# Small operations of an attention from VectorE to ScalarE and GpSimd

## The chip, the cores and the metric

One core of a Trainium2 chip runs the whole kernel. Its engines are TensorE (PE in the profile; PEld is its weight load), VectorE (DVE), ScalarE (ACT), GpSimd (POOL) and SyncE (SP, which only starts transfers here). Each engine works through its own queue in order; the engines wait for each other through semaphores. The metric is the device time of one execution in microseconds, and lower is better.

## The reference

The kernel computes one decoder block for 512 positions of width 1024 in float32:

```python
h  = rmsnorm(x);  P = h @ W_in        # A: [B, C, x_in]; B: [q, k/v per branch, branch gates]; merge gates gA, gB
yA = B * causal_dwconv3(C * x_in)
yB = NSA(q, compressed / selected / window keys)
x  = x + W_o( sigmoid(gA) * (yA @ W_A) + sigmoid(gB) * (yB @ W_B) )
x  = x + W_down( silu(causal_dwconv3(W_g rmsnorm(x)) + b) * (W_u rmsnorm(x)) )
```

The attention (NSA) has 8 heads in 2 groups of 4. For each head three softmaxes are taken over the same query and added, each times a gate of its own (a sigmoid for each position, head and branch): one over compressed keys, one over selected blocks, one over a window. With 512 positions all blocks are selected and the window covers everything, so the last two are plain causal attentions. The compressed keys are blocks of 32 positions taken every 16 positions. A position sees a block that has ended at or before it:

```python
def masked_softmax(s, mask):
    p = jax.nn.softmax(jnp.where(mask, s, NEG), axis=-1)
    return jnp.where(mask, p, 0.0)
```

The first 31 positions see no block at all: all their scores are `NEG`, the softmax is even, and the second `where` makes it zero.

## The kernel before

**Products.** Every float32 operand of a large product is cut into a high part (a rounded copy, made by ScalarE) and a low part (what the rounding left). TensorE then adds three products: high by high, high by low, low by high. In the profile these are lines L420, L421 and L423 of the helper `dense`. The low part of a weight comes in one of three ways, chosen by `by` in `load_w` (L130 to L146): VectorE subtracts (`"vector"`), GpSimd subtracts (`"pool"`), or, with `"dma"`, ScalarE writes a negated copy of the high part and an accumulating transfer on GpSimd's queue adds the weight to it (`dma_split`, L165 to L170).

**Stages.** The token projections, the compressed keys and the preparation of queries and keys come first, then the attention with the short convolution and the merge gates between, then the output product, then the feed-forward part, which takes from about 370 us to the end.

**The attention.** `attend` runs for each pair of a query tile of 128 positions (tiles 3, 2, 1, 0) and a group of four heads: eight times. In each, TensorE makes the scores of each head (L639/L640; L665 for tile 0), VectorE adds the causal mask and takes the maximum (L691, L692), ScalarE takes exponentials with a running sum (L693), VectorE inverts the sums and multiplies them by the gates (`scale_of`, L642 to L644), ScalarE scales the exponentials (L699), VectorE transposes 32x32 blocks (L626), and two transfers on SyncE's queue carry them out to DRAM (`td_e`, L632) and back in transposed order (`tn_e`, L634). Then ScalarE and GpSimd split them into high (`ph`, L725) and low parts (L726), and TensorE multiplies them with the values (`po`, L728, L733). The tile for the exponentials (`e`) has two buffers, so a third use waits until the first has been read out.

**The compressed branch** sits between. Its scores for four heads and 32 blocks are gathered in `xc`, 128 positions x 128. VectorE takes the maximum (L704), subtracts it (L705), ScalarE takes the exponential (L706), VectorE sums (L707), inverts and multiplies by the gate (`scale_of`), GpSimd multiplies by a table of visible blocks `cm_one` (L709) and by the scale (L710), ScalarE makes the high part (L712), VectorE the low part (`xs`, L713), and TensorE transposes both (`ptc`, L716).

**Work between.** `conv_tile` (four times, three weights each: `wr_a`, `wh_a`, `wl_a`) and `mix_a_pair` and `gate_tile` (weights `wr_g` and `wr_ao`, low parts by GpSimd, L145) stand behind the attention in the text. They depend on little, and TensorE gets them as filling.

**Order.** The text gives only dependencies and priorities. A planner simulates the engines with its own costs when the kernel is built, and writes one fixed order for each queue, the queues of transfers among them. On the chip nothing is reordered: where a planned duration is not met, what stands behind waits. An edit can therefore move instructions of other parts, too.

Of the kernel before, what the change touches and what calls it, by code (L numbers as in the profile page):

```python
# [11 lines left out]
F32 = mybir.dt.float32  # L12
F32R = mybir.dt.float32r
I32 = mybir.dt.int32
AF = mybir.ActivationFunctionType
ALU = mybir.AluOpType
AX = mybir.AxisListType

P = 128
# [4 lines left out]
H = 8  # L24
# [61 lines left out]
def tile_block(ctx: ExitStack, tc: tile.TileContext, xT, pos, par, par2, w_tok, w_a3, w_gate, w_ao, w_bo, w_o,  # L86
# [13 lines left out]
    def const(shape, name, dt=F32, pool=sb):  # L100
        return pool.tile(shape, dt, name=name, tag=name)
# [262 lines left out]
                            pattern=[[-1, P]], channel_multiplier=1)  # L364
    cm_add = const([P, NT, NC], "cm_add", F32, pb)
    nc.gpsimd.memset(cm_add, 0.0)
    cm_one = const([P, NT, NC], "cm_one", F32, pb)
    nc.gpsimd.memset(cm_one, 1.0)
    for m, f in ((cm_add, NEG), (cm_one, 0.0)):
        nc.gpsimd.affine_select(out=m, in_=m, compare_op=ALU.is_ge, fill=f, base=-(CMPB - 1),  # L370
                                pattern=[[P, NT], [-STRIDE, NC]], channel_multiplier=1)
    mhalf = const([P, 12], "mhalf")
    nc.gpsimd.memset(mhalf, -0.5)

# [163 lines left out]
    def values(tt, acc):  # L538
        r = r1[:, tt:tt + 1]
        vv = acc[:, 0:256].rearrange("p (h d) -> p h d", d=HD)  # L540
        nc.scalar.activation(v_t[:, tt, :, 0:HD], vv, AF.Copy, scale=r)
        nc.vector.scalar_tensor_tensor(v_t[:, tt, :, HD:], vv, r, v_t[:, tt, :, 0:HD].bitcast(F32),
                                       op0=ALU.mult, op1=ALU.subtract)
        gt = gate_n[:, tt, :]
        nc.scalar.activation(gt, acc[:, 256:280], AF.Tanh, scale=r1h[:, tt:tt + 1])
        nc.vector.tensor_scalar(gt, gt, 0.5, 0.5, op0=ALU.mult, op1=ALU.add)

    kh = kHH.rearrange("p (b g) s -> p b g s", g=G)
    nc.gpsimd.tensor_copy(kh[:, 1, :, 0:NC], warm[:, 1:2, None].to_broadcast([P, G, NC]))
# [58 lines left out]
    def attend(pt_, g, qt):  # L608
# [32 lines left out]

        def scale_of(sums, br):  # L642
            nc.vector.reciprocal(sums, sums)
            nc.vector.tensor_mul(sums, sums, gates[:, :, br:br + 1])  # L644

        xc = small("xc", NC)
        if off == 0:
# [8 lines left out]
        if qt == 0:  # L656

            e = e_tile("", 2)
            mx = pt_.tile([P, HG, 2], F32, name=f"mx{tag}", tag="mx", bufs=1)
            sums = small("sums", 2)  # L660
            for i in range(HG):
                sc = s_bank(f"sc{tag}{i}")
                w = sc[:, 0:2 * (NC + P)].rearrange("p (b k) -> p b k", b=2)
                for j in range(2):
                    nc.tensor.matmul(w, q[:, g * HG + i, :], kk5[:, j, :, g, 0:NC + P], start=j == 0, stop=j == 1)  # L665
                nc.vector.tensor_add(xc[:, i, :], w[:, 0, 0:NC], cm_add[:, qt, :])
                dg = w[:, :, NC:]
                nc.vector.tensor_tensor(dg, dg, causal[:, None, :].to_broadcast([P, 2, P]), op=ALU.add)
                nc.vector.tensor_reduce(mx[:, i], dg, axis=AX.X, op=ALU.max, negate=True)
                for br in (1, 0):  # L670
                    nc.scalar.activation(e[:, :, br, i], dg[:, br].rearrange("p (b i) -> p b i", i=SQ), AF.Exp,
                                         bias=mx[:, i, br:br + 1], accum_out=sums[:, i, br:br + 1])
            nc.vector.reciprocal(sums, sums)
            nc.vector.tensor_mul(sums, sums, gates[:, :, 1:3])
            for br in (1, 0):
                nc.vector.tensor_tensor(e[:, :, br], e[:, :, br],
                                        sums[:, None, :, br:br + 1].to_broadcast([P, QB, HG, SQ]), op=ALU.mult)
            turned = turn(e, 2)
        for br in (1, 0):
            if qt > 0:  # L680
                o = off if br == 0 else 0
                e = e_tile(br, qt + 1)
                mx = small(f"mx{br}", 1)
                sums = small(f"sums{br}", 1)
                for i in range(HG):
                    sc = s_bank(f"sc{tag}{i}{br}")
                    scores(sc[:, 0:o + nk], i, br, NC - o, NC + nk)
                    if o:
                        nc.vector.tensor_add(xc[:, i, :], sc[:, 0:NC], cm_add[:, qt, :])
                    dg = sc[:, o + nk - P:o + nk]  # L690
                    nc.vector.tensor_add(dg, dg, causal)  # L691
                    nc.vector.tensor_reduce(mx[:, i], sc[:, o:o + nk], axis=AX.X, op=ALU.max, negate=True)  # L692
                    nc.scalar.activation(e[:, :, :, i].rearrange("p b k i -> p k b i"),  # L693
                                         sc[:, o:o + nk].rearrange("p (k b i) -> p k b i", b=QB, i=SQ), AF.Exp,
                                         bias=mx[:, i], accum_out=sums[:, i])
                scale_of(sums, 1 + br)
                for i in range(HG):
                    v = e[:, :, :, i]
                    nc.scalar.activation(v, v, AF.Copy, scale=sums[:, i])  # L699
                turned = turn(e, qt + 1)  # L700
            if br == 0:
                mcs = small("mcs", 2)
                mc, sc_ = mcs[:, :, 0:1], mcs[:, :, 1:2]
                nc.vector.tensor_reduce(mc[:, :, 0], xc, axis=AX.X, op=ALU.max)  # L704
                nc.vector.tensor_tensor(xc, xc, mc.to_broadcast([P, HG, NC]), op=ALU.subtract)  # L705
                nc.scalar.activation(xc, xc, AF.Exp)  # L706
                nc.vector.reduce_sum(sc_[:, :, 0], xc, axis=AX.X)  # L707
                scale_of(sc_, 0)
                nc.gpsimd.tensor_tensor(xc, xc, cm_one[:, qt, None, :].to_broadcast([P, HG, NC]), op=ALU.mult)  # L709
                nc.gpsimd.tensor_tensor(xc, xc, sc_.to_broadcast([P, HG, NC]), op=ALU.mult)  # L710
                xs = small("xs", 2 * NC, F32R)
                nc.scalar.activation(xs[:, :, 0:NC], xc, AF.Copy)  # L712
                nc.vector.tensor_sub(xs[:, :, NC:], xc, xs[:, :, 0:NC].bitcast(F32))  # L713
                pt = t_bank(f"ptc{tag}", 0)
                for a in range(2):
                    nc.tensor.transpose(pt[:, a * P:(a + 1) * P],  # L716
                                        xs[:, 2 * a:2 * a + 2, :].rearrange("p h c -> p (h c)").bitcast(F32), ident)
                pc = pt_.tile([P, 2, P], F32R, name=f"pc{tag}", tag="pc", bufs=1)
                nc.scalar.activation(pc, pt[:, 0:2 * P].rearrange("p (a t) -> p a t", a=2), AF.Copy)
            k0 = br if qt == 0 else 0  # L720
            for kt in range(qt + 1):
                pl = turned[:, :, kt + k0]
                pt = pl.bitcast(F32)
                ph = pt_.tile([P, QB, P], F32R, name=f"ph{tag}{kt}{br}", tag="pth", bufs=NPT)
                nc.scalar.activation(ph, pt, AF.Copy)  # L725
                nc.gpsimd.tensor_sub(pl, pt, ph.bitcast(F32))  # L726
                w = v_t[:, kt, 2 * br + g, :]
                nc.tensor.matmul(acc4, w, ph, start=kt == 0 and br == 1, stop=False)  # L728
                if kt == 0 and br == 0:
                    for b in range(2):  # L730
                        nc.tensor.matmul(by_head(acc, b), vc_t[:, b, g, :], pc.rearrange("p a (q i) -> p a q i", i=SQ),
                                         start=False, stop=False)
                nc.tensor.matmul(acc4, w, pl, start=False, stop=kt == qt and br == 0)  # L733
# [24 lines left out]
    def conv_tile(i):  # L758
        accs = []
        for j in (1, 2, 0):  # L760
            w = load_w(w_a3[2 + 3 * i + j], D, f"a{i}{j}", by="dma" if 3 * i + j > 1 else "vector")
            acc = d_bank(f"pa{i}{j}")
            dense(acc, w_units(w, xg_h, xg_l, KD))
            if j == 1:
                cs_ = f_tile(f"cs{i}")[:, 0:S]
                nc.vector.tensor_mul(cs_, acc, r1sq)
            elif j == 2:
                u = f_tile(f"u{i}")
                nc.gpsimd.memset(u[:, 0:2], 0.0)
                nc.vector.tensor_mul(u[:, 2:], acc, cs_)  # L770
                t = f_tile(f"ct{i}")[:, 0:S]
                causal_conv(t, u, par_sb[:, CAW + 3 * i:CAW + 3 * i + 3])
                nc.gpsimd.tensor_mul(t, t, r1b)
            else:
                nc.vector.tensor_mul(t, acc, t)
                nc.scalar.activation(ya_h[:, i, :], t, AF.Copy)
                nc.vector.tensor_sub(ya_l[:, i, :], t, ya_h[:, i, :].bitcast(F32))
# [371 lines left out]
```

## Time and profile before

| | us |
|---|---|
| median of 3 runs | 711.18 (710.22 to 711.29) |
| the profiled execution | 714.02 |
| its span, from first to last instruction | 712.3 |
| TensorE busy | 696.3 |
| VectorE busy | 544.1 |
| ScalarE busy | 432.4 |
| GpSimd busy | 234.3 |

The profile shows one execution. The times are from the start of its span. In a group of instructions stand the line, the engine, the operation, output <- input by the program's names, the shape, the count, then busy time in us and the mean of one in ns, and behind the bar the idle time of the engine before them and who ended it. "PE x <- DVE y: 3.9, 2, 2.0" says that TensorE waited for VectorE's y for 3.9 us in all, twice, 2.0 at the longest. In the timeline the first number is the start in us, the second the duration, and brackets hold the engine's idle time just before. The granted TensorE clock was 0.998 of full speed over the span.

### The profile page before, as it was taken

How to read it: one execution, taken by the hardware profiler on the slowest of the kernel's cores; microseconds unless marked ns; L12 is line 12 of the kernel's file. 1: busy time of each engine (PE TensorE's matmuls, PEld its weight loads, DVE VectorE, ACT ScalarE, POOL GpSimd, SP SyncE). 2: the span in 40 equal slices, each digit the busy share in tenths (PEclk: the TensorE clock that was granted, in tenths of full speed). 3: DMA queues.
4: the chain of work that ended last, by engine and by line, in shares of the span. 5: the costliest groups of instructions: out<-in, count | busy, mean ns of one | idle time of the engine just before them, and what ended most of it. 6: DMA issues, size and time to landing. Idle time of an engine off the chain costs nothing.

```text
span 712.3 us, 11270 instructions
## 1 busy us (share of the span) xinstructions
PE 696.3 (98%) x4125; PEld 617.6 (87%) x4125; DVE 544.1 (76%) x932; ACT 432.4 (61%) x722; POOL 234.3 (33%) x219
## 2 busy tenths in 40 slices
PE   9999899988999998999999999999999999999997
PEld 9999777766888786888889999899999999999986
DVE  6887775868878889365895799998787877878643
ACT  7535465847888866522776767676555665646440
POOL 3051422246878767633012221221111222112110
PEclk9999999999999999999999999999999999999999
DMA  7333587688787645445386798987878779785675
GB/s 274 98 95 119 146 179 151 159 252 225 234 225 229 182 157 148 174 139 181 102 213 119 175 232 197 229 209 185 208 182 215 184 175 208 187 194 104 125 140 149
DMA packets 56599, 126.44 MB, mean 178 GB/s; under 512 B 5088, under 2 KB 20576, under 8 KB 56544
## 3 DMA queue, kind: packets, MB, share of 16 engines
q1 hardware_dynamic: 41984, 91.39, 40.5%
q0 software_dynamic: 14272, 34.08, 27.8%
q8 instruction: 32, 0.52, 0.3%
q10 hardware_dynamic: 288, 0.26, 0.1%
q14 instruction: 23, 0.19, 0.1%
HBM read 113.13 MB, written 12.58 MB: 176 GB/s over the span
## 4 chain that ended last, share of the span: by engine, by line
PE 85%; DVE 6%; DMA 4%; ACT 3%; POOL 1%; issue 1%; SPq 0%; ACTq 0%; DVEq 0%
PE p L421 9%; PE p L420 9%; PE p L423 9%; PE pdn L421 6%; PE pdn L420 6%; PE pdn L423 6%; PE pg L421 3%; PE pg L420 3%; PE pg L423 2%; PE pa L423 2%; PE po L420 2%; PE po L421 2%; PE po L423 2%; PE pa L420 2%; PE pa L421 2%; PE pj_s L264 2%
## 5 line engine op out<-in xcount | busy, mean ns | idle before, releaser
L421 PE MATMUL p<-xf_l,sh 128*128 128x256 f32 x336 | 80.6, 277 | 0.0
L420 PE MATMUL p<-xf_h,sh 128*128 128x256 f32 x336 | 80.5, 277 | 0.0
L170 POOL DMA_DIRECT2D wl_s<-in_w_ff_dram x22 | 19.5, 885 | 167.3 <-ACT wl_s L169 155.6
L162 ACT ACTIVATE sh<-s 128x1024 fp32r<-128x1024 f32 x44 | 46.2, 1057 | 37.9 <-PE p L421 24.7
L421 PE MATMUL pdn<-al,wh_d 128*128 128x512 f32 x176 | 68.7, 391 | 0.0
L420 PE MATMUL pdn<-ah,wh_d 128*128 128x512 f32 x176 | 68.5, 390 | 0.0
L421 PEld LDWEIGHTS p<-xf_l,sh 128*128 128x128 f32 x336 | 63.0, 188 | 0.1
L420 PEld LDWEIGHTS p<-xf_h,sh 128*128 128x128 f32 x336 | 63.0, 188 | 0.1
L726 POOL TENSOR_TENSOR tn_e<-tn_e,ph 128x512 fp32r<-128x512 f32 x40 | 52.0, 1311 | 30.7 <-ACT ph L725 29.9
L163 DVE TENSOR_TENSOR sl<-s,sh 128x1024 fp32r<-128x1024 f32 x44 | 53.5, 1218 | 8.7 <-ACT sh L162 8.7
L168 ACT ACTIVATE wh_s<-wr_s 128x1024 fp32r<-128x1024 f32 x22 | 23.3, 1058 | 53.6 <-PE pdn L421 50.1
L170 POOL DMA_DIRECT2D wl_d<-in_w_dn_dram x22 | 26.5, 1203 | 77.2 <-ACT wl_d L169 69.2
L423 PE MATMUL p<-xf_h,sl 128*128 128x256 f32 x336 | 51.5, 277 | 0.0
L420 PE MATMUL pg<-xg_h,wh_g 128*128 128x512 f32 x128 | 50.2, 392 | 0.0
L421 PE MATMUL pg<-xg_l,wh_g 128*128 128x512 f32 x128 | 50.0, 390 | 0.0
L423 PE MATMUL pdn<-ah,wl_d 128*128 128x512 f32 x176 | 47.7, 389 | 0.0
L1068 DVE TENSOR_TENSOR x<-x,pdn 128x512 f32<-128x512 f32 x48 | 32.7, 682 | 16.3 <-PE pdn L423 15.5
L423 PEld LDWEIGHTS p<-xf_h,sl 128*128 128x128 f32 x336 | 44.5, 188 | 0.2
L145 POOL TENSOR_TENSOR wl_g<-wr_g,wh_g 128x1024 fp32r<-128x1024 f32 x16 | 38.4, 2398 | 8.5 <-PE pa L423 6.1
L420 PE MATMUL p<-xf_h,wh_s 128*128 128x256 f32 x168 | 40.5, 276 | 0.0
L421 PE MATMUL p<-xf_l,wh_s 128*128 128x256 f32 x168 | 40.5, 276 | 0.0
L423 PEld LDWEIGHTS pdn<-ah,wl_d 128*128 128x128 f32 x176 | 33.0, 188 | 6.9
(360 smaller groups left out, 2122.1 us busy)
## 6 DMA issues: line engine op xcount, KB each, us to landing
wr_s<-in_w_ff_dram SPq DMA_DIRECT2D x44, 512.0 KB, 5.3
wl_s<-in_w_ff_dram POOLq DMA_DIRECT2D x22, 512.0 KB, 7.8
wr_d<-in_w_dn_dram SPq DMA_DIRECT2D x22, 512.0 KB, 7.4
wl_d<-in_w_dn_dram POOLq DMA_DIRECT2D x22, 512.0 KB, 8.8
wr_g<-in_w_gate_dram SPq DMA_DIRECT2D x16, 512.0 KB, 4.6
wr_a<-in_w_a_dram SPq DMA_DIRECT2D x12, 512.0 KB, 3.7
tl<-in_w_ff_dram POOLq DMA_DIRECT2D x22, 256.0 KB, 7.4
wl_a<-in_w_a_dram POOLq DMA_DIRECT2D x10, 512.0 KB, 7.8
```

The source lines that it names most:

```text
L145: e.tensor_sub(lo[:, 0:n], raw[:, 0:n], hi[:, 0:n].bitcast(F32))
L162: hi = nc.scalar.activation(h, v, AF.Copy)
L163: nc.vector.tensor_sub(l, v, h.bitcast(F32))
L168: nc.scalar.activation(h, raw, AF.Copy)
L170: nc.gpsimd.dma_start(l if dst is None else dst, src, accum_op=ALU.add)
L264: nc.tensor.matmul(acc, xg_h[:, k, ts_], wh, start=k == 0, stop=False)
L420: nc.tensor.matmul(acc, wh, xh, start=first and i == 0, stop=False)
L421: nc.tensor.matmul(acc, wh, xl, start=False, stop=False)
L423: nc.tensor.matmul(acc, wl, xh, start=False, stop=last and i == len(units) - 1)
L726: nc.gpsimd.tensor_sub(pl, pt, ph.bitcast(F32))
L1068: nc.vector.tensor_add(xj, xj, acc)
```

## The change

It has five parts. (1) The product of the inverted sums with the gates goes from VectorE to GpSimd, in `scale_of` and in the part for query tile 0. (2) The softmax of the compressed branch: the maximum comes out negated, and ScalarE takes the exponential of each of the four heads separately, with the maximum as bias and the sum as a second output, in place of a subtraction and a sum on VectorE and one exponential. (3) The table `cm_one` goes, with the product by it. What it did for blocks that a position does not see, the exponential does already, since their scores are `NEG` below the maximum; for positions 0 to 30, which see no block, the gate of this branch is set to zero by a fill on GpSimd in `values`. (4) The low part of the compressed weights, `xs`, goes from VectorE to GpSimd. (5) The last of the four convolution tiles has its three low parts by GpSimd's subtraction in place of the accumulating transfer.

```diff
     cm_add = const([P, NT, NC], "cm_add", F32, pb)
     nc.gpsimd.memset(cm_add, 0.0)
-    cm_one = const([P, NT, NC], "cm_one", F32, pb)
-    nc.gpsimd.memset(cm_one, 1.0)
-    for m, f in ((cm_add, NEG), (cm_one, 0.0)):
-        nc.gpsimd.affine_select(out=m, in_=m, compare_op=ALU.is_ge, fill=f, base=-(CMPB - 1),
-                                pattern=[[P, NT], [-STRIDE, NC]], channel_multiplier=1)
+    nc.gpsimd.affine_select(out=cm_add, in_=cm_add, compare_op=ALU.is_ge, fill=NEG, base=-(CMPB - 1),
+                            pattern=[[P, NT], [-STRIDE, NC]], channel_multiplier=1)
...
         nc.vector.tensor_scalar(gt, gt, 0.5, 0.5, op0=ALU.mult, op1=ALU.add)
+        if tt == 0:
+            g3 = gt.rearrange("p (h b) -> p h b", b=3)[:, :, 0]
+            nc.gpsimd.affine_select(out=g3, in_=g3, compare_op=ALU.is_ge, fill=0.0, base=-(CMPB - 1),
+                                    pattern=[[0, H]], channel_multiplier=1)
...
             nc.vector.reciprocal(sums, sums)
-            nc.vector.tensor_mul(sums, sums, gates[:, :, br:br + 1])
+            nc.gpsimd.tensor_mul(sums, sums, gates[:, :, br:br + 1])
...
             nc.vector.reciprocal(sums, sums)
-            nc.vector.tensor_mul(sums, sums, gates[:, :, 1:3])
+            nc.gpsimd.tensor_mul(sums, sums, gates[:, :, 1:3])
...
-                nc.vector.tensor_reduce(mc[:, :, 0], xc, axis=AX.X, op=ALU.max)
-                nc.vector.tensor_tensor(xc, xc, mc.to_broadcast([P, HG, NC]), op=ALU.subtract)
-                nc.scalar.activation(xc, xc, AF.Exp)
-                nc.vector.reduce_sum(sc_[:, :, 0], xc, axis=AX.X)
+                nc.vector.tensor_reduce(mc[:, :, 0], xc, axis=AX.X, op=ALU.max, negate=True)
+                for i in range(HG):
+                    nc.scalar.activation(xc[:, i], xc[:, i], AF.Exp, bias=mc[:, i], accum_out=sc_[:, i])
                 scale_of(sc_, 0)
-                nc.gpsimd.tensor_tensor(xc, xc, cm_one[:, qt, None, :].to_broadcast([P, HG, NC]), op=ALU.mult)
                 nc.gpsimd.tensor_tensor(xc, xc, sc_.to_broadcast([P, HG, NC]), op=ALU.mult)
                 xs = small("xs", 2 * NC, F32R)
                 nc.scalar.activation(xs[:, :, 0:NC], xc, AF.Copy)
-                nc.vector.tensor_sub(xs[:, :, NC:], xc, xs[:, :, 0:NC].bitcast(F32))
+                nc.gpsimd.tensor_sub(xs[:, :, NC:], xc, xs[:, :, 0:NC].bitcast(F32))
...
-            w = load_w(w_a3[2 + 3 * i + j], D, f"a{i}{j}", by="dma" if 3 * i + j > 1 else "vector")
+            w = load_w(w_a3[2 + 3 * i + j], D, f"a{i}{j}", by="pool" if i == 3 else "dma" if 3 * i + j > 1 else "vector")
```

## The prediction

> **What bounds the kernel now.** I read the busy shares first, then who TensorE waited for, then the chain that ended last and the waits in order of time. TensorE sets the end: it is busy for all but 16 us, and 1.1 us of that lies before the first matmul.
>
> ```profile
> PE 696.3 (98%) x4125; PEld 617.6 (87%) x4125; DVE 544.1 (76%) x932; ACT 432.4 (61%) x722; POOL 234.3 (33%) x219
> ```
>
> Columns of the next view: who waited <- for whom: us in total, times, longest.
>
> ```profile
> PE ptc L716 <- DVE xs L713: 3.9, 2, 2.0
> PE pa L423 <- DMA wl_a<-in_w_a_dram: 2.1, 2, 1.9
> PE sc L639 <- ACT e L693: 2.0, 4, 1.1
> PE po L728 <- ACT ph L725: 1.8, 2, 1.3
> PE wu L193 <- POOL ones L188: 1.1, 1, 1.1
> PE ptc L716 <- DVE xc L666: 0.7, 1, 0.7
> ```
>
> So the change can win little: these lines, without the first load (wu), sum to 10.5 us, and 8.4 of it (ptc, sc, po) is the attention. The matmuls, which the change leaves alone, keep their time. Where the waits stand (start, us, engine, line):
>
> ```profile
> 148.92 0.50 PE L639 MATMUL sc<-kk,qT 128*128 128x512 f32 x1 [1.13 <-ACT e L693]
> 154.80 0.50 PE L728 MATMUL po<-ph,v_t 128*128 128x512 f32 x1 [1.25 <-ACT ph L725]
> ...
> 168.02 0.41 PE L716 MATMUL ptc<-ident,xs 128*128 128x128 f32 x2 [1.90 <-DVE xs L713]
> ```
>
> Now the reason for the last one. GpSimd and VectorE in that stretch:
>
> ```profile
> 164.91 2.81 POOL L145 TENSOR_TENSOR wl_ao<-wr_ao,wh_ao 128x1024 fp32r<-128x1024 f32 x1
> ...
> 165.64 2.24 DVE L713 TENSOR_TENSOR xs<-xc,xs 128x128 fp32r<-128x128 f32 x1
> ```
>
> The 128x128 subtraction on VectorE starts at 165.64 and ends at 167.88, just after the GpSimd subtraction ends (164.91 + 2.81 = 167.72). It does not compute for 2.24 us; it is held while GpSimd runs. The spread of the same instruction says so too (min/median/max ns, first and last start), and the groups (busy us, mean ns) show that every VectorE operation with two SBUF inputs pays:
>
> ```profile
> L713 DVE TENSOR_TENSOR xs<-xc,xs x8: 270/892/2240, 136.1 to 281.6; 128x128 fp32r<-128x128 f32 x8
> L644 DVE TENSOR_TENSOR sums<-sums,gate_n x12: 163/872/1619, 128.9 to 254.8; 128x4 f32<-128x4 f32 x12
> ```
> ```profile
> L644 DVE TENSOR_TENSOR sums<-sums,gate_n 128x4 f32<-128x4 f32 x12 | 10.0, 836 | 0.3
> L713 DVE TENSOR_TENSOR xs<-xc,xs 128x128 fp32r<-128x128 f32 x8 | 8.5, 1062 | 0.8 <-ACT xs L712 0.8
> L644 DVE TENSOR_TENSOR mcs<-mcs,gate_n 128x4 f32<-128x4 f32 x8 | 7.6, 955 | 0.1
> L705 DVE TENSOR_TENSOR xc<-xc,mcs 128x128 f32<-128x128 f32 x8 | 7.4, 927 | 0.0
> ```
>
> Free, the subtraction takes 0.27 us and the 128x4 product 0.16; on the mean they take 1.06 and 0.84. The four groups hold VectorE for 33.5 us. Nearly all of that falls into the attention, where VectorE is the fullest engine after TensorE (busy us in the order PE, PEld, DVE, ACT, POOL, then the granted clock and the DMA share):
>
> ```profile
> 220.00:240.00 20.00, 20.00 (x96) 16.23 (x95) 17.43 (x41) 16.39 (x43) 16.28 (x14) 1.00 0.77 223
> ...
> 160.00:280.00 120.00, 115.72 (x534) 94.03 (x533) 100.84 (x215) 94.30 (x232) 90.44 (x69) 1.00 0.69 203
> ```
>
> **The change part by part.** *Off VectorE.* The four groups leave it: 33.5 us against 100.8 busy of 120 us in that stretch. Masked scores, row maxima and transposes behind them on VectorE come forward. That itself frees no TensorE time; only the waits above do.
>
> *Onto GpSimd.* It takes over 22 small products (the 20 above and the two 128x8 ones of the first query tile) and eight 128x128 subtractions, and loses the eight products with the table. The rows (busy us, mean ns):
>
> ```profile
> L726 POOL TENSOR_TENSOR tn_e<-tn_e,ph 128x512 fp32r<-128x512 f32 x40 | 52.0, 1311 | 30.7 <-ACT ph L725 29.9 <-PE sc L640 0.7
> L145 POOL TENSOR_TENSOR wl_g<-wr_g,wh_g 128x1024 fp32r<-128x1024 f32 x16 | 38.4, 2398 | 8.5 <-PE pa L423 6.1 <-ACT wh_g L143 2.4
> ...
> L709 POOL TENSOR_TENSOR xc<-xc,cm_one 128x128 f32<-128x128 f32 x8 | 4.1, 510 | 8.0 <-DVE mcs L707 8.0
> L710 POOL TENSOR_TENSOR xc<-xc,mcs 128x128 f32<-128x128 f32 x8 | 3.2, 406 | 1.0 <-DVE mcs L644 0.5 <-PE po L731 0.5
> ```
>
> A 128x128 subtraction there is priced like the product L710, 0.41 us. A 128x4 product has no row on GpSimd: at least VectorE's 0.16, at most L710's 0.41; I take 0.3, nearer to L710, since it is the same engine. Sum: 22 x 0.3 + 8 x 0.41 - 4.1 = +5.8 us (2.7 to 8.2) on an engine that is busy 90.4 of 120 us: it fits. What hurts is the queue. GpSimd works in order, and a small product can stand behind a weight's low part (2.40 us) or an L726 (1.31). But VectorE already pays that: being held until the GpSimd instruction ends is the same wait. What differs is that GpSimd's turn is part of the order that the planner writes, while the hold shows in the trace as unplanned: TensorE stands at ptc with other matmuls queued behind it.
>
> The three waits at ptc (3.9 + 0.7 = 4.6 us) are thus the first term. Bounds: all gone, -4.6; or each is replaced by a full low part in front of the subtraction, 3 x 2.40 = 7.2, so +2.6. I take the two long ones as gone (-3.9) and half a low part (+1.2) as new: **-2.7**.
>
> The Trainium skill (GPSIMD Engine Reference, Engine selection) speaks against this part: two-input elementwise work belongs on VectorE, since GpSimd takes about twice as long. The rows agree on free instructions (0.41 against 0.27 us, a factor of 1.5); by that rule three subtractions in front of ptc would add 3 x 0.27, or 0.8 us as an estimate from that page. But against the held instruction (mean 1.06 us) the rows favour GpSimd, so I don't follow it.
>
> *Onto ScalarE.* Each of eight heads' groups swaps one exponential for four with a running sum; VectorE's maximum now comes negated. Prices: the old one as a group, the new ones from the 128x128 exponentials with a sum, which follow each other:
>
> ```profile
> L706 ACT ACTIVATE xc<-xc 128x128 f32<-128x128 f32 x8 | 2.4, 302 | 1.0 <-DVE xc L705 1.0
> ```
> ```profile
> 262.32 0.37 ACT L671 ACTIVATE e<-sc,mx 128x128 f32<-128x128 f32 x1
> ...
> 262.68 0.36 ACT L671 ACTIVATE e<-sc,mx 128x128 f32<-128x128 f32 x1
> ```
>
> That is 0.36 us a piece with its sum read out; for 128x32 it is no more than that and no less than a fourth of 0.30. I take 0.36: 4 x 0.36 - 0.30 = +1.1 us for each group, +9 us in all (0 at the lower end), on an engine at 94.3 of 120 us. It also loses three 128x1024 copies of the convolution tile. TensorE's waits for ScalarE outside the two places around 150 are 0.9 + 0.5 = 1.4 us (sc 2.0 - 1.13; po 1.8 - 1.25). Bounds: all gone, -1.4, to double, +1.4; I take **+0.5**, because ScalarE is the only engine whose work in the attention grows without losing a hold.
>
> *The last convolution tile.* Three weights get their low part by a GpSimd subtraction (2.40 us each) in place of a second copy and an accumulating transfer. Two of these are issued while the first attention result is on its way through DRAM:
>
> ```profile
> 133.62 0.88 POOL L170 DMA_DIRECT2D wl_a<-in_w_a_dram  x1 [1.74 <-ACT wl_a L169]
> ...
> 137.99 0.86 POOL L170 DMA_DIRECT2D wl_a<-in_w_a_dram  x1 [3.37 <-ACT wl_a L169]
> ```
> ```profile
> 137.73 10.25 DMA td_e<-e
> ```
> ```profile
> td_e<-e SPq DMA_DIRECT2D x16, 256.0 KB, 5.4
> ```
>
> The way out took 10.25 us on the chain, where such a piece takes 5.4 us from issue to landing on the median. Both waits around 150 (1.13 at 148.92, 1.25 at 154.80) follow it: the buffer for the next exponentials is free only then, and the way back starts only then. Without the accumulating transfers it can land up to 4.85 us earlier, more than both waits. Bounds: 0, if the loads that stay fill the gap, to -2.4. I take **-2.4**. The subtractions hold GpSimd for 7.2 us where it had little to do.
>
> *The table and the gates.* The table is built in the first microseconds and read only by L709: nothing on the path. In its place one fill of 128x8 gates stands on GpSimd, at most as long as the 128x128 fill:
>
> ```profile
> L370 POOL TENSOR_SCALAR_AFFINE_SELECT cm_one<-cm_one x1: 314/314/314, 3.7 to 3.7; 128x128 f32<-128x128 f32 x1
> ```
> ```profile
> 69.61 4.55 POOL L377 TENSOR_TENSOR qst<-qst,mhalf 128x6 f32<-128x6 f32 x2 [13.04 <-DVE qst L561]
> ```
> ```profile
> 81.79 3.65 PE pa L423 x8
> ...
> 127.91 1.81 PE pa L423 x8
> ```
>
> GpSimd was idle for 13 us before 69.61, so the fill costs 0. If it lands behind the two powers, the transfer for the weight awaited at 81.79 goes out 0.31 us later and adds that. I leave that wait (1.9 us) as it is: it lies ahead of the changed attention. It also shows the price of a bad gap: the eight matmuls after it took 3.65 us instead of 1.81.
>
> Sum: -2.7 + 0.5 - 2.4 = **-4.6 us**. The profiled execution took 714.02 us (span 712.3, 1.72 around it), 2.84 above the median of the runs, 711.18. The same step off the median gives **706.6 us**.
>
> **The rivals.** *All waits of the attention go*: -4.6 - 1.4 - 2.4 = -8.4, **702.8 us**. For it: TensorE has matmuls of gates to fill with, as between 220 and 240, where it is busy throughout. Against it: its order is fixed, and other misjudged durations stay (the remaining VectorE products next to GpSimd).
>
> *Nothing moves*: the waits wander to other places, since the plan of the whole attention is made anew, and the first td_e is as late as before because loads move up into the free queue; **711.2 us**, within 1.4. For it: TensorE is at 98%, and idle time of VectorE costs nothing.
>
> *GpSimd's queue takes the place of the hold, and it is slower.* The subtraction before ptc and the scale of the exponentials are planned behind a low part each; the three places cost 7.2 instead of 4.6, and the scale, up to 2.40 us late instead of 0.84, uses up what td_e gained: +2.6, **713.8 us**. It decides once the mean delay at the three places passes 4.6 / 3 = 1.5 us. One gap that halves the clock as at 81.79 would add another 1.84. For it: at 164.91 such a low part started just ahead of the subtraction. Against it: a planner that knows GpSimd's 2.40 us puts other matmuls in front.
>
> The Trainium skill (TensorE: Matmul & The Clock Gate, Part 1) puts the drop to the slow clock behind an idle window of about 3.4 us; here 1.9 us went before it at 81.79, while the 1.90 us at 168.02 had no such cost. By the page the 1.84 would not be due.
>
> *It doesn't do what it says*: without the table, rows that see no block would be wrong unless their gate is zero; that changes no time.
>
> **How the numbers follow.** A measurement of this kernel can tell about 0.2%, 1.4 us, from no change. Chances: forecast 0.54, all waits gone 0.14, nothing moves 0.14, queue 0.18. The range goes from 702.3, just under the second case, to 713.5, just short of the last case's price, which leaves most of that case and a little below outside. Faster: 0.14 and nearly all of 0.54, 0.67. Same: 0.14 and the rest, 0.15. Slower: 0.18.
>
> **What would show it.** Right: no VectorE product of 128x4 and no 128x128 subtraction in the groups; VectorE some 30 us less busy; td_e from the first group under 8 us on the chain; TensorE's waits on xs and on ph under half of theirs. Wrong: ptc waiting for GpSimd's xs for over 4 us, TensorE waiting for low parts of gate weights, or for exponentials for over 3 us. The wait at 81.79 gone or doubled would mean that the plan changed ahead of the attention, which I have not counted.

## The result and the profile after

The changed kernel takes 699.92 us (median of 4 runs, 699.28 to 701.74) against 711.10 before (4 runs): a ratio of 0.9849 (95% interval 0.9829 to 0.9870), 11.2 us faster. The forecast was 706.6; the sign was right, the time lies below the range. The profiled execution took 700.20 us, its span is 698.5.

The page's line of busy times, after:

```profile
PE 690.7 (99%) x4125; PEld 616.7 (88%) x4125; DVE 508.3 (73%) x886; ACT 436.8 (63%) x775; POOL 242.6 (35%) x240
```

TensorE is idle for 7.8 us of its span, 8.2 less than before. Its busy time has fallen too, by 5.6 us, though it does the same matmuls. Whom it waits for, after:

```profile
PE po L727 <- ACT ph L724: 1.8, 2, 1.7
PE wu L193 <- POOL ones L188: 1.1, 1, 1.1
PE pj_s L264 <- ACT wh_t L162: 0.6, 1, 0.6
PE ph L474 <- ACT qT L589: 0.3, 1, 0.3
```

All waits at ptc, at sc and for the weight's transfer (pa) are gone. The sum at po, on ph, is 1.8 us as before, but it stands elsewhere: 0.16 us at the first po (1.25 at 154.80 before) and 1.67 at 172.97. In the stretch from 160 to 280 us (columns as before):

```profile
160.00:280.00 120.00, 118.33 (x557) 99.13 (x556) 70.72 (x175) 97.09 (x268) 94.22 (x86) 1.00 0.66 202
```

VectorE is 30.1 us less busy there, ScalarE 2.8 and GpSimd 3.8 us more. The moved operations by group, GpSimd then ScalarE:

```profile
L712 POOL TENSOR_TENSOR xs<-xc,xs 128x128 fp32r<-128x128 f32 x8 | 3.7, 464 | 1.5 <-ACT xs L711 1.4
L645 POOL TENSOR_TENSOR sums<-sums,gate_n 128x4 f32<-128x4 f32 x12 | 2.8, 237 | 2.1 <-DVE sums L644 1.9
L645 POOL TENSOR_TENSOR mcs<-mcs,gate_n 128x4 f32<-128x4 f32 x8 | 2.3, 293 | 1.3 <-DVE mcs L644 1.3
```
```profile
148.41 0.31 ACT L707 ACTIVATE xc<-xc,mcs 128x32 f32<-128x32 f32 x1
...
148.71 0.31 ACT L707 ACTIVATE xc<-xc,mcs 128x32 f32<-128x32 f32 x1
```

And the first attention result on its way out, on the chain that ended last:

```profile
134.44 5.23 DMA td_e<-e
139.76 6.24 DMA tn_e<-td_e
```

It took 10.25 us before. By the profile alone, all but one of the signs named as "right" are there (the wait on ph has not halved), and the gain is more than twice the forecast. The experiments had to say what each part brought.

### The profile page after: what moved, and what is told of

Same layout as the page of the kernel before. It is cut to its first block, busy times and chain, and to the rows that moved or that the text cites. A ratio compares the mean times of both kernels' runs of the same rounds, so it can differ in the third digit from the quotient of the medians.

```text
span 698.5 us, 11286 instructions
## 1 busy us (share of the span) xinstructions
PE 690.7 (99%) x4125; PEld 616.7 (88%) x4125; DVE 508.3 (73%) x886; ACT 436.8 (63%) x775; POOL 242.6 (35%) x240
## 4 chain that ended last, share of the span: by engine, by line
PE 89%; DMA 5%; ACT 2%; DVE 1%; issue 1%; SPq 0%; ACTq 0%
PE p L418 10%; PE p L417 10%; PE p L420 10%; PE pdn L418 6%; PE pdn L417 6%; PE pdn L420 6%; PE pg L417 4%; PE pg L418 4%; PE pg L420 4%; PE po L418 2%; PE po L417 2%; PE po L420 2%; DMA tn_e<-td_e 2%; PE pa L417 2%; PE pa L418 2%; PE pj_s L264 2%
```

## The experiments

Each run was timed against the kernel before on the same chip (medians of before: 710.77 to 711.57 on four chips). Edits are against the kernel before unless said otherwise.

| run | median us | ratio to before (95%) |
|---|---|---|
| conv_only | 701.82 | 0.9868 (0.9845 to 0.9890) |
| tile3_vector | 702.94 | 0.9893 (0.9874 to 0.9912) |
| dummy_tiny | 704.08 | 0.9888 (0.9842 to 0.9934) |
| before_tiny | 705.04 | 0.9906 (0.9875 to 0.9936) |
| same_plan_plain | 707.02 | 0.9937 (0.9914 to 0.9960) |
| plain_loads | 708.26 | 0.9951 (0.9929 to 0.9973) |
| undo_conv | 708.62 | 0.9973 (0.9958 to 0.9989) |
| gates_only | 709.86 | 0.9992 (0.9976 to 1.0008) |
| fill_only | 710.03 | 0.9985 (0.9971 to 1.0000) |
| tile2_only | 710.66 | 0.9984 (0.9966 to 1.0003) |
| dummy_plain | 712.18 | 1.0011 (0.9999 to 1.0023) |
| dummy_transfers | 712.63 | 1.0028 (1.0011 to 1.0046) |
| unheld_vector | 714.89 | 1.0052 (1.0035 to 1.0068) |
| all_pool | 702.44 | 0.9866 (0.9821 to 0.9910) |

### Which part carries it

**conv_only**: part 5 of the change alone.

```diff
-            w = load_w(w_a3[2 + 3 * i + j], D, f"a{i}{j}", by="dma" if 3 * i + j > 1 else "vector")
+            w = load_w(w_a3[2 + 3 * i + j], D, f"a{i}{j}", by="pool" if i == 3 else "dma" if 3 * i + j > 1 else "vector")
```

> The kernel before with only the last convolution tile's low parts by GpSimd. If the transfers were what held the first attention result, td_e on the chain falls from 10.25 to 5 to 7 us, the two waits near 150 go, and it is 2.4 us faster than before: 708.7. If the loads that stay fill the gap, 711. If this part carries most of the whole change, 704 or less.

It took 701.82, 9 of the 11 us. td_e took 4.61 us on the chain. Of the two waits near 150, the one at sc went, but the first one at po did not:

```profile
147.84 0.50 PE L728 MATMUL po<-ph,v_t 128*128 128x512 f32 x1 [1.91 <-ACT ph L725]
```

**undo_conv** is the other half: the changed kernel with that line as it was.

```diff
-            w = load_w(w_a3[2 + 3 * i + j], D, f"a{i}{j}", by="pool" if i == 3 else "dma" if 3 * i + j > 1 else "vector")
+            w = load_w(w_a3[2 + 3 * i + j], D, f"a{i}{j}", by="dma" if 3 * i + j > 1 else "vector")
```

> The changed kernel with the last convolution tile put back to accumulating transfers; the gate products, the softmax per head, the fill and the low part of xs stay changed. If the transfers beside the first attention result carry the gain, td_e takes about 10 us again and the time goes back to 707 to 710. If the other four parts carry a good half of it together (VectorE is some 30 us less busy), it stays at 705 or below.

It took 708.62, with td_e at 9.93 us again: the other four parts, with 30 us less on VectorE, bring 2 us (0.27%) together. The two halves add up to the whole. **gates_only** moves just the 22 products:

```diff
-            nc.vector.tensor_mul(sums, sums, gates[:, :, br:br + 1])
+            nc.gpsimd.tensor_mul(sums, sums, gates[:, :, br:br + 1])
...
-            nc.vector.tensor_mul(sums, sums, gates[:, :, 1:3])
+            nc.gpsimd.tensor_mul(sums, sums, gates[:, :, 1:3])
```

> The kernel before with only the 22 gate products on GpSimd. If the holds count, VectorE loses 17.9 us of busy time, and the time falls by 2 to 4 us: 707 to 709. If GpSimd's queue delays the scale as much as the hold did, within 1 us of 711. The price of the 128x4 product on GpSimd is about 0.25 us.

Not to be told from no change, with VectorE at 522.7 us busy in place of 544.1. Its waits show why that bought nothing:

```profile
PE po L728 <- ACT ph L725: 5.5, 4, 2.1
PE pa L423 <- DMA wl_a<-in_w_a_dram: 1.6, 2, 1.1
```

The ones at ptc are gone, and ph is awaited for 5.5 us instead of 1.8. The softmax and the low part of xs were not run alone. **fill_only** adds the gate fill and keeps everything else:

```diff
         nc.vector.tensor_scalar(gt, gt, 0.5, 0.5, op0=ALU.mult, op1=ALU.add)
+        if tt == 0:
+            g3 = gt.rearrange("p (h b) -> p h b", b=3)[:, :, 0]
+            nc.gpsimd.affine_select(out=g3, in_=g3, compare_op=ALU.is_ge, fill=0.0, base=-(CMPB - 1),
+                                    pattern=[[0, H]], channel_multiplier=1)
```

> The kernel before with the gate fill of the first tile added and nothing else (the table stays, so the fill is redundant). The written order of every engine is that of before with one instruction more. If the wait at 81.79 and the slow clock behind it (1.86 + 1.84 us) stand in every execution of before and the fill is what ended them, it is 3.7 us faster than before: 707.4. If they belonged to that one profiled execution, or go for another reason, it is within 1 us of before: 711. The two powers in front of the transfer then show whether they take 4.55 us or about 2.7.

No gain clear of noise. The early wait is still there in its profile, without the slow clock behind it:

```profile
81.48 2.11 PE L423 MATMUL pa<-xg_h,wl_a 128*128 128x512 f32 x8 [1.77 <-DMA wl_a<-in_w_a_dram]
```

So the 3.65 us for these matmuls belonged to that one execution of before, and the wait varies: in same_plan_plain (below), whose engines do the same work in the same order as before, it is 0.20 us. That fits the 2.84 us by which that execution stood above the median.

### Are VectorE's holds the cost?

**unheld_vector** meant to take the holds away without moving anything:

```diff
-            nc.vector.tensor_mul(sums, sums, gates[:, :, br:br + 1])
+            for i in range(HG):
+                nc.vector.tensor_scalar(sums[:, i], sums[:, i], gates[:, i, br:br + 1], None, op0=ALU.mult)
...
-                nc.vector.tensor_tensor(xc, xc, mc.to_broadcast([P, HG, NC]), op=ALU.subtract)
+                for i in range(HG):
+                    nc.vector.tensor_scalar(xc[:, i], xc[:, i], mc[:, i], None, op0=ALU.subtract)
```

> The kernel before with the 128x4 products of scale_of and the subtraction of the maximum kept on VectorE but written as one instruction per head with a single SBUF tensor and a per-partition scalar, so that no second SBUF tensor is read. Nothing moves to GpSimd or ScalarE. If the gain comes from taking the holds away (25 us of VectorE in these groups before), VectorE's product takes about 0.16 us everywhere, VectorE is some 15 us less busy, and the time falls by 2 to 4 us: 707 to 709. If the gain needs the move to other engines, or is that of the transfers alone, the time stays within 1 us of 711.

It was 0.5% slower, and it did only half of what it was for. The products are no longer held (169 to 214 ns each), but there are four for each group, so they take 0.8 us as before. The new subtraction, with one SBUF tensor, is held as well (min/median/max ns):

```profile
L707 DVE TENSOR_SCALAR xc<-xc,mcs x32: 227/466/2430, 124.1 to 278.4; 128x32 f32<-128x32 f32 x32
```

It takes up to 2.43 us, the length of a low part on GpSimd, and 21.8 us in all where the old one took 7.4. VectorE is busy for 547.9 us, 3.8 more than before, so as a test of the holds the run is void. The better test came unasked, in conv_only. Its xs groups and waits:

```profile
L713 DVE TENSOR_TENSOR xs<-xc,xs 128x128 fp32r<-128x128 f32 x8 | 9.6, 1195 | 2.8 <-ACT xs L712 2.6
```
```profile
PE po L728 <- ACT ph L725: 2.7, 2, 1.9
PE wu L193 <- POOL ones L188: 1.1, 1, 1.1
PE sc L639 <- ACT e L693: 0.5, 1, 0.5
PE ph L477 <- ACT qT L588: 0.3, 1, 0.3
PE pj_s L264 <- ACT wh_t L162: 0.2, 1, 0.2
```

There xs stays on VectorE and is held longer than before (mean 1.20 us against 1.06), and TensorE does not wait at ptc at all. A hold alone does not make a wait.

### Are the transfers the cost?

**tile3_vector** takes the same transfers away and gives GpSimd nothing:

```diff
-by="dma" if 3 * i + j > 1 else "vector")
+by="dma" if 1 < 3 * i + j < 9 else "vector")
```

> The kernel before with the last tile's low parts by VectorE (1.22 us each) in place of the accumulating transfers. GpSimd gets nothing. If taking the transfers away is what counts, td_e takes 5 to 7 us and the time is 701 to 705, in spite of 3.7 us more on VectorE. If GpSimd's part in it counts, or one particular order, it stays above 707.

702.94: it needs no GpSimd. **tile2_only** takes as many transfers away, earlier:

```diff
-by="dma" if 3 * i + j > 1 else "vector")
+by="pool" if i == 2 else "dma" if 3 * i + j > 1 else "vector")
```

> The kernel before with the third convolution tile in place of the last by GpSimd's subtraction; the last keeps its transfers. The written order of TensorE, VectorE and SyncE is exactly that of before; on GpSimd and ScalarE only the changed instructions differ. As many transfers and ScalarE copies go as in the run with the last tile alone, but some 25 us earlier, when no attention result is on its way. If the collision with td_e matters, td_e stays near 10 us and the time within 1.5 us of 711. If fewer transfers or fewer copies anywhere are what helps, it comes to 702 to 706.

No gain. On the chain td_e still took 9.23 us. Its TensorE, VectorE and SyncE work in the order of before, and the waits at ptc stand as before (3.9 + 0.7 us). It matters which transfers go: those beside the attention results.

**dummy_transfers** keeps them, unread, beside GpSimd's subtraction; **dummy_tiny** does so with 8 of 512 columns:

```diff
             w = load_w(w_a3[2 + 3 * i + j], D, f"a{i}{j}", by="pool" if i == 3 else "dma" if 3 * i + j > 1 else "vector")
+            if i == 3:
+                for hf in range(2):
+                    dm = f_tile(f"dm{j}{hf}")[:, 0:S]
+                    nc.scalar.activation(dm, raws["a3%d" % j][:, hf * S:(hf + 1) * S], AF.Copy, scale=-1.0)
+                    nc.gpsimd.dma_start(dm, w_a3[2 + 3 * i + j][:, hf * S:(hf + 1) * S], accum_op=ALU.add)
```

> The kernel before with the last tile's low parts by GpSimd, as in the run with that part alone, but the negated copies and the accumulating transfers of the same bytes are kept (in halves of 256 KB), into tiles that nobody reads. TensorE waits for none of them. If their load on the DMA engines holds td_e, it takes 8 us or more and the time is 708 to 711. If TensorE's wait for the weights through them was the cost, it is 702 to 704.

> The run with dummy transfers again, with the same negated copies and as many accumulating transfers on GpSimd's queue into tiles that nobody reads, but each of them moves 8 columns of 512 (1/64 of the bytes). If the load on the DMA engines is what cost 10.8 us there (712.6 against 701.8 without), this one is 701 to 704. If the instructions cost it (copies on ScalarE, issues on GpSimd) or the order that they lead to, it stays above 708.

They took 712.63 and 704.08. TensorE waits for none of the transfers, yet with the full bytes all of the gain is lost, and with 1/64 of them most of it is back; copies and issues are the same. It was not a long td_e that cost it, though. In dummy_transfers I had expected 8 us or more, and on the chain stands:

```profile
134.86 6.22 DMA td_e<-e
```

The planner, which sees the bytes, wrote different orders for the two: in dummy_transfers one near that of before, with waits at ptc (3.4 + 0.7 us) and 4.6 us at sc; in dummy_tiny one without any wait at ptc. So this pair does not part the load from the order. **before_tiny** cuts the transfers of the kernel before in the same way (`l[:, 0:8]`, `src[:, 0:8]` for the last tile):

> The kernel before with its accumulating transfers for the last convolution tile cut to 8 of 1024 columns (the low parts of that tile are then wrong beyond them: that part of the computation is left out). Copies, issues and TensorE's wait for the transfer stay; GpSimd subtracts nothing. If the bytes in flight beside the attention result count, it is 701 to 705, near the run with the last tile alone (701.8), with a third order of the instructions. If GpSimd's or VectorE's subtraction is needed for the gain, it stays above 708.

It took 705.04, without any subtraction. **plain_loads** puts plain loads of the same 1.5 MB on ScalarE's queue in place of the dummies (`nc.scalar.dma_start(dm, ...)`, no copies):

> The kernel before with the last tile's low parts by GpSimd and, beside them, the same 1.5 MB of weights loaded once more by plain transfers from ScalarE's queue into tiles that nobody reads. If the bytes count, whoever moves them, it is 707 to 712. If it was the accumulating kind of transfer, which reads its destination too and is issued by GpSimd, it is 701 to 704.

It took 708.26, between both: with plain bytes about two thirds of the gain are lost, in an order of its own again, and with td_e at 6.21 us on the chain.

### The load, or the plan?

All these runs but tile2_only changed TensorE's order as well as the chip's load. **same_plan_plain** and **dummy_plain** drop the addition and nothing else:

```diff
-        nc.gpsimd.dma_start(l if dst is None else dst, src, accum_op=ALU.add)
+        nc.gpsimd.dma_start(l if dst is None else dst, src)
```

(in the first for the last tile's weights alone, in the second for the dummies). The written order of all five queues stays that of the kernel before, or of dummy_transfers.

> The kernel before with the last tile's three accumulating transfers made plain (they overwrite instead of adding, so that tile's low parts are wrong: the addition is left out). The written order is the same on all five queues. A plain transfer writes without reading its destination, so only what the chip does in that one plan changes. If the gain of 9 us is the load that the chip bears, td_e falls below 8 us and the time to 703 to 707. If it is the plan that the planner makes once the transfers are gone, the time stays within 1.5 us of 711.

> The run with dummy transfers (712.6) with those transfers made plain; the written order is the same on all five queues and nothing that is read changes. If the load on the chip is the cost, 703 to 708. If the plan is, within 1.5 us of 712.6.

Neither theory is right alone. In the order of before, lighter transfers bring 4.5 us (707.02). In the order of dummy_transfers they bring nothing that can be told (712.18), so there the kind of transfer is not what costs; that the order does is likely, but that order was not run without the bytes. SyncE's queue shows the first, from the start of td_e to that of tn_e, in before and then in same_plan_plain:

```profile
135.10 4.79 SPq L632 DMA_DIRECT2D td_e<-e  x4
139.99 2.38 SPq L139 DMA_DIRECT2D wr_ao<-in_w_ao_dram  x1
148.07 0.38 SPq L634 DMA_DIRECT2D tn_e<-td_e  x1
```
```profile
131.64 3.44 SPq L635 DMA_DIRECT2D td_e<-e  x4
135.18 0.82 SPq L139 DMA_DIRECT2D wr_ao<-in_w_ao_dram  x1
141.24 0.38 SPq L637 DMA_DIRECT2D tn_e<-td_e  x1
```

13.0 us became 9.6. TensorE's waits in same_plan_plain:

```profile
PE ptc L719 <- DVE xs L716: 3.9, 2, 2.0
PE wu L196 <- POOL ones L191: 1.1, 1, 1.1
PE ptc L719 <- DVE xc L669: 0.7, 1, 0.7
PE po L731 <- ACT ph L728: 0.5, 1, 0.5
```

po has fallen from 1.8 to 0.5 and sc from 2.0 to 0.2; the 3.9 + 0.7 us at ptc stand to the tenth as before. So the waits on the attention's result follow the load. Those at ptc go with the written order: they stand in every run that keeps the order of before, and are gone in conv_only, but also in gates_only and undo_conv, which have the accumulating transfers and gain 2 us or less. dummy_plain has the waits at ptc (3.4 + 0.7) too, and TensorE's order there is nearly that of before.

conv_only gains 4.4 us more than same_plan_plain. The spans of the two profiled executions differ by 4.3 us (705.3 and 701.0): in conv_only TensorE is idle for 2.9 us less (4.6 less at ptc, 2.2 more at po) and busy for 1.4 us less, while TensorE ran at half clock for 3.4 us of same_plan_plain's execution (from 162.6) and not in conv_only's attention. Two things changed between them, the order and the transfers that are gone and not only lighter. No run parts these two: conv_only's order with the transfers in it was not run.

### Further along the same way

**all_pool** is the changed kernel with the other accumulating transfers of the convolution gone as well:

```diff
-by="pool" if i == 3 else "dma" if 3 * i + j > 1 else "vector")
+by="pool" if 3 * i + j > 1 else "vector")
```

> The changed kernel with the other seven accumulating transfers of the convolution weights also replaced by GpSimd's subtraction (2.4 us each; GpSimd is busy for 28 of the 80 us from 60 to 140). The transfer that TensorE awaited at 81.79 before is one of them. If that wait (0 to 1.9 us from execution to execution) and the clock behind it go, the time falls by 0.5 to 2 us under the changed kernel: 698 to 699.5. If GpSimd's subtractions then delay the scales of the normalised heads in front of the attention, it is 701 or more.

702.44, a ratio of 0.9866 against 0.9849 for the change: no better. The early wait on the weight is not in its profile, but neither is it in that of the changed kernel, while 1.3 us come at pqt, for VectorE's part of the keys, and po has 2.5 against 1.8.

## Why the prediction was right or wrong

**The last convolution tile (-2.4): the step that failed. The mechanism held in part, the size did not.** I said that the accumulating transfers hold td_e and that two waits follow it. td_e did fall, to 5.23 us. But I priced the term by the two waits that name td_e's followers, with everything behind them left where it stood, and it measured 9.0 us (conv_only). The 6.6 us between are all that the forecast missed. With lighter transfers in an unchanged order the gain is 4.5 (same_plan_plain): the waits at sc and po fell by 3.1 us, more than the 2.4 of the two places, and what the other 1.4 are made of is not shown. The rest, 4.4, came with the transfers gone altogether and with the order that the planner writes without them. There the waits did not go as I said: sc fell from 2.0 to 0.5, but po rose from 1.8 to 2.7, and what went were the 4.6 at ptc. I named a new plan only as the way in which nothing moves.

**The waits at ptc (-2.7): the size nearly right, the cause in part.** I put them down to VectorE's hold at xs and had them go with the move to GpSimd. The hold is real, and at those places it ends last. But it is not enough: in conv_only xs stays, is held longer and nobody waits, and gates_only, which keeps xs on VectorE and the transfers too, has no wait at ptc either. Whether a hold costs TensorE time depends on what the order put behind it. A run without the holds in an unchanged order is missing, so their own price stays open. The four parts that were to earn this term and to cost +0.5 on ScalarE, -2.2 together, bring 2 us (undo_conv). That this comes out so near is partly luck: the waits at ptc went whole, and po took some of it back (1.8 to 3.2 us). 22 fewer held products alone bring nothing measurable.

**The prices** were close. GpSimd's 128x4 product takes 0.24 to 0.29 us (0.3 taken), its 128x128 subtraction 0.46 (0.41), four exponentials follow each other at 0.30 us (0.36 taken), so ScalarE grows by 0.9 us for each group instead of 1.1. VectorE lost 30.1 of the 33.5 us in that stretch. None of these decided anything. The +0.5 for ScalarE cannot be seen: the waits on it fell.

**The wait at 81.79** was left as it is. It is a matter of the execution: 1.86 us in before, 1.77 in fill_only, 0.20 in same_plan_plain, none in conv_only, and with it goes a good part of the profile's 2.84 us above the median. Taking the step off the median was right for that reason.

**The rivals.** "All waits go", 702.8, was nearest, and the range stopped just under it because I took the waits that the profile names for all there was to win, the matmuls keeping their time. TensorE's busy time fell by 5.6 us beside them; 1.84 is the slow clock of that execution, and what the rest is made of stays open. "Nothing moves" did not come: part 5 alone is far outside it. "GpSimd's queue takes the place of the hold" did not happen: the products do not queue up (GpSimd was idle for 2.1 and 1.3 us before the two groups, mostly for VectorE's reciprocal) and ptc has none. By the rule of the Trainium skill (GPSIMD Engine Reference, Engine selection), that part should have cost time; free, the subtraction is 1.7 times as long as VectorE's (0.46 against 0.27 us), which agrees, and the kernel is none the slower for it.

## What to carry to other kernels

A transfer that holds a result on the critical chain can be worth more than the waits that name it: here 4.5 us against 2.4 with the order unchanged, and twice that with the transfer gone and the order that the planner wrote without it. Before crediting a move between engines with a wait, look for the same held instruction in a run where nobody waits for it. To part a resource's load from the plan's luck, change what a transfer does (its kind) without changing what the planner sees.

## What the runs showed of the hardware

- Accumulating and plain transfers of the same bytes, in the same order (before, then same_plan_plain, both from 128 to 152 us; median us from issue to landing):

```profile
wl_a<-in_w_a_dram POOLq DMA_DIRECT2D x2, 512.0 KB, 9.0
```
```profile
wl_a<-in_w_a_dram POOLq DMA_DIRECT2D x2, 512.0 KB, 5.5
```

- VectorE's tensor-by-scalar instruction with a single SBUF tensor is held by GpSimd up to 2.43 us (unheld_vector, on 128x32), which I had not expected; on 128x1 it was not (80 products, 169 to 214 ns). The Trainium skill (SBUF — State Buffer, Who interferes with whom) counts this instruction among those that can take both ports and so contend; the trace agrees for 128x32.
- GpSimd's two powers ahead of the early transfer take 4.55 us together in some executions and 2.7 in others at the same place in the order: here before and, for the other case, the changed kernel. tile3_vector had the long form, tile2_only the short one. What decides is open.

```profile
69.61 4.55 POOL L377 TENSOR_TENSOR qst<-qst,mhalf 128x6 f32<-128x6 f32 x2 [13.04 <-DVE qst L561]
```
```profile
69.64 1.36 POOL L374 TENSOR_TENSOR qst<-qst,mhalf 128x6 f32<-128x6 f32 x1 [2.00 <-DVE qst L562]
71.45 1.36 POOL L374 TENSOR_TENSOR qst<-qst,mhalf 128x6 f32<-128x6 f32 x1 [0.45 <-DVE qst L562]
```

- The eight matmuls after a gap of 1.86 us ran at half speed in one execution (3.65 us), and after 1.77 us in another they did not (2.11). The Trainium skill's idle window of about 3.4 us (TensorE: Matmul & The Clock Gate, Part 1) is longer than the gap that was followed by the drop. The half speed comes in spells of 3.41 us and in other executions at other places: at 148.5 us in fill_only, 162.6 in same_plan_plain, 173.3 in dummy_plain (two on end). The length of a gap does not decide alone: the wait at ptc of 1.90 us in before had no spell behind it, the same wait of 1.88 us in same_plan_plain had one. In the 3.41 us ahead of the spell TensorE had been idle for 1.9 us in before and for 2.0 to 2.4 in the other three, in pieces or at once; but unheld_vector had a spell after 1.3 us, so no threshold comes out of it. The times of before go with the clock: the 10 of its 72 executions beside the experiments that had a clock of 1.000 took 710.3 us (median), the 22 with 0.995 took 712.4.
